# Low part of the second low-rank product: 128 rows of both operands in place of 64

## The chip, the core and the metric

The kernel runs on one core of one Trainium2 chip. A core has five engines that work side by side: TensorE (matrix products, in the profile PE, with its weight loads as PEld), VectorE (DVE), ScalarE (ACT), GpSimd (POOL) and SyncE (SP), which issues the transfers. The metric is the device time of one execution in microseconds, the median of several runs. The profile is one further execution, taken with the hardware profiler.

## The reference, cut to what matters

The reference is one step of a two-layer backbone for 640 tokens (128 context tokens, 512 latent tokens) of width 1024. Layer 0 mixes tokens with a gating MLP, layer 1 with a bidirectional RWKV-7 scan; each is followed by an MLP. The change touches layer 1, where decay and in-context rate are made by two low-rank products for each direction `d`:

```python
z = w0[i, d] + tanh(xw @ w1[i, d]) @ w2[i, d]          # w1: 1024 x 64, w2: 64 x 1024
decay = exp(-exp(-softplus(-z) - 0.5))
a = sigmoid(a0[i, d] + (xa @ a1[i, d]) @ a2[i, d])      # a1: 1024 x 64, a2: 64 x 1024
```

The second product of each, `... @ w2` and `... @ a2`, has an inner size of 64. Its result, for all 1024 channels and 640 tokens, goes into the scan together with `r`, `k` and `v`.

## The kernel before, in words

Activations lie with channels on the 128 partitions, so width 1024 is 8 tiles of 128 channels (two heads each) by 640 tokens. A product in float32 is made of products of two rounded parts: each operand is split into a high part and the rest, the low part, and high by high, high by low and low by high are summed in PSUM. `split` (lines 85 to 90) and `fill` (98 to 101) do so: ScalarE copies to the rounded type, VectorE subtracts.

`rwkv_project` (line 749) makes what the scan needs. The first low-rank products (lines 790 to 795) give, for each kind, 128 rows: 64 of direction 0 and 64 of direction 1. `hidden` (806 to 816) makes of them one operand `hw` per direction with 128 rows. For direction 0 rows 0 to 63 hold the high part and rows 64 to 127 the low part of the same 64 values; for direction 1 the halves change places. The second weights come from the host with their 64 rows written twice (line 1989), so that a tile `l2` has the same 64 rows in both halves.

`lora2` (895 to 915) makes the second products for one channel tile `t`. ScalarE rounds the weights to `hi` (898) and VectorE makes the low part `lo` (899), both on all 128 rows. Then, for each direction, kind (`tw` decay, `ta` rate) and half of 320 tokens, two products go into one bank of PSUM: line 911, `hi` by `hw` on 128 rows, which is high by high and high by low in one, and line 912, `lo` by `hw` on those 64 rows that hold the high part. Line 913 takes the bank out on ScalarE with a tanh (`ACT tw L913` and `ACT ta L913` in the profile). The pool `pv` has two such banks (line 869). `lora2` is a generator, and its steps are put between other products.

The loop of the stage (1046 to 1082) goes over `t` = 0 to 8. One turn starts `lora2`, makes the products of `r` for tile t (`rmm`, 48 matmuls at line 114, out to `rps`) and those of `v` for an earlier part (`vmm`, 60 matmuls at line 1038, out to `vps`), with the steps of `lora2` between, and then `finish` (978), which spreads the norms of `k` by a product (line 981, `rbps`), makes `kk` (985) and calls `prep` (917) for both directions: from `tw` a running sum on VectorE (920, 921), exponentials on ScalarE (927, 929), small copies on GpSimd (932), the products `KR` (938, 940) and `IT` (947, 950, 952), stored to DRAM for the scan. The pool `ep` has two buffers for `tw` and three for `ta` (870), so a `tw` can be written only when line 952 has read the one of the same direction of the tile before.

Into the same stage GpSimd puts the first part of the scan: a substitution of 31 steps (lines 1128 and 1130), released three steps at a time by `next(core)` and `core.send` (995, 1017) between the instructions of `finish`.

The order on each engine is not that of the code line by line. The framework orders the instructions ahead of time by priority and by when it takes each to be ready, with costs of its own for each instruction; `high_priority` blocks move some ahead. On the chip every engine then works through its own queue in that order and waits on semaphores. Transfers are issued on SyncE's queue.

Of the kernel before, what the change touches and what calls it, by code (L numbers as in the profile page):

```python
# [28 lines left out]
def tile_trunk(ctx: ExitStack, tc: tile.TileContext, a: dict):  # L29
# [3 lines left out]
    pe = nc.tensor  # L33
# [709 lines left out]
    def fl(x):  # L743
        return x.rearrange("p c t -> p (c t)")
# [4 lines left out]
    def rwkv_project(norm, dr, PC, bon, unwind, core, ATs, go):  # L749
        with ExitStack() as es:  # L750
# [19 lines left out]
            for hf, (t0, t1) in enumerate(HS):  # L770
                x0, x1 = XS[hf]
                a0, a1 = max(x0, 1), min(x1, T - 1)
                with urgent(hf):
                    bc = norm.rstd(hf)
                    for k in range(KT):
                        h, x = hs[k], xx[k]
# [13 lines left out]
                for j, w, ps in zip((1, 4, 5), lws, pl):  # L790
                    for k in range(KT):
# [3 lines left out]
                                  start=(k == 0), stop=(k == KT - 1))  # L795
# [99 lines left out]
            def lora2(raw, tiles):  # L895
                hi = ev_.tile([P, 4, P], F32R, "lh", "l2h")
                lo = ev_.tile([P, 4, P], F32R, "ll", "l2l")
                act.copy(hi.rearrange("p a b -> p (a b)"), raw[:, 0:512])
                vec.tensor_tensor(out=lo.rearrange("p a b -> p (a b)"), in0=raw[:, 0:512],
                                  in1=hi.rearrange("p a b -> p (a b)"), op=ALU.subtract)  # L900
                yield
                for d in range(2):
                    a0 = 64 * d
                    for x, tag in enumerate(("tw", "ta")):
                        z = ep.tile([P, 10, 64], F32, tag, tag)
                        tiles[d, x] = z
                        hw = hid[x][d]
                        for h in range(2):
                            sl = slice(320 * h, 320 * h + 320)
                            ps = pv.tile([P, 512], F32, "z", "zps")[:, 0:320]  # L910
                            pe.matmul(ps, hi[:, 2 * x + d], hw[:, sl], start=True, stop=False)
                            pe.matmul(ps, lo[a0:a0 + 64, 2 * x + d], hw[a0:a0 + 64, sl], start=False, stop=True)
                            act.activation(out=fl(z)[:, sl], in_=ps, func=AF.Tanh, scale=0.5,  # L913
                                           bias=hb[:, 2 * x + d, tiles["t"]:tiles["t"] + 1])
                            yield
# [130 lines left out]
            for t in range(KT + 1):  # L1046
                z = iter(())
                if t < KT:
                    tiles = {"t": t}
                    rl, rr = nxt  # L1050
                    z = lora2(rl, tiles)
                    next(z)
                    rk = rmm(t, rr, z)
                    if t == 0:
                        khat()
                    if t < KT - 1:
                        nxt = ahead(t + 1)
# [801 lines left out]
    for h in range(2):  # L1859
        a0 = 64 * h  # L1860
# [162 lines left out]
```

## Time and profile before

| | us |
|---|---|
| median of 3 runs (2079.52 to 2081.85) | 2079.96 |
| profiled execution, its own time | 2069.75 |
| span in that profile, first to last instruction | 2067.9 |
| TensorE busy in the span | 1938.2 |
| VectorE busy | 1344.3 |
| ScalarE busy | 842.3 |
| GpSimd busy | 543.9 |
| first and last start of the products of lines 911 and 912 | 824.7 to 1043.7 |

The granted clock of TensorE over the span was 0.944 of full speed. A row of a group gives line, engine, operation, what is written and read, the shape (partitions by elements), and a count, then busy us and mean ns, or, for one tile, minimum, median and maximum ns. A row of the timeline gives the start in us from the start of the span, a length in us and, in brackets, idle time of the engine just before and what ended it. Matmuls overlap in part, so two starts in a row say more than a length. A few of the matmuls are missing from the records.

### The profile page before, as it was taken

To read this page: it belongs to the slowest core of one execution; us is meant where nothing else is said; L and a number is where in the kernel's file an instruction comes from. 1 tells how busy PE (TensorE), PEld (TensorE's weight loads), DVE (VectorE), ACT (ScalarE), POOL (GpSimd) and SP (SyncE) were. 2 spreads that over 40 slices of the span, in tenths; PEclk is the share of its full clock that TensorE was granted. 3 is DMA by queue.
4 is the path that set the end of the run, shared out by engine and by line. 5 is a ranking of instruction groups with operands and counts; after the bars stand their busy time and mean duration, and the time that the engine had idled before them with its cause. 6 is when DMAs were issued, how large, how long until landed. Compare 5 with 4: busy or idle time off the path is not lost.

```text
span 2067.9 us, 39399 instructions
## 1 busy us (share of the span) xinstructions
PE 1938.2 (94%) x15594; PEld 1685.9 (82%) x15594; DVE 1344.3 (65%) x2652; ACT 842.3 (41%) x1945; POOL 543.9 (26%) x793
## 2 busy tenths in 40 slices
PE   6999999999999879898869999999999999999997
PEld 4766999999999759777757766767787899999997
DVE  5444556746465696776787587787757666556564
ACT  5322442413233245554524545454434633333241
POOL 0000003213020110377642284465301023121210
PEclk9999999999999889998778999998799999999999
DMA  8777121241413114454564445452241221312121
GB/s 283 267 259 249 62 72 61 82 143 62 153 54 129 63 65 156 126 172 145 175 192 141 151 145 172 158 174 67 77 132 57 92 75 59 102 62 92 64 80 52
DMA packets 124441, 254.60 MB, mean 123 GB/s; under 512 B 24416, under 2 KB 63968, under 8 KB 124128
## 3 DMA queue, kind: packets, MB, share of 16 engines
q1 hardware_dynamic: 123824, 251.62, 37.6%
q8 instruction: 123, 2.02, 0.4%
q14 instruction: 62, 0.51, 0.1%
q10 hardware_dynamic: 432, 0.46, 0.1%
HBM read 214.67 MB, written 45.22 MB: 126 GB/s over the span
## 4 chain that ended last, share of the span: by engine, by line
PE 78%; DVE 11%; ACT 4%; issue 3%; POOL 3%; DMA 1%; SPq 0%; DVEq 0%; ACTq 0%; POOLq 0%
PE fmps L114 27%; PE fmps L611 13%; PE zps L311 5%; PE p L1197 4%; PE wops L1467 4%; PE vps L1038 3%; PE za L1326 2%; PE za L1313 2%; PE rps L114 2%; PE sy L1340 2%; DVE slo L453 1%; PE sy L1321 1%; PE trps L1219 1%; PE adaps L1453 1%; DVE cs L603 1%
## 5 line engine op out<-in xcount | busy, mean ns | idle before, releaser
L611 PE MATMUL fmps<-th,shi 128*128 128x320 f32 (+2 forms) x1208 | 270.5, 312 | 9.8 <-ACT th L561 4.1
L284 DVE SCALAR_TENSOR_TENSOR x<-fmps,mod,x 128x128 f32<-128x128 f32 (+2 forms) x153 | 74.7, 527 | 254.1 <-PE fmps L114 254.1
L611 PEld LDWEIGHTS fmps<-th,shi 128*128 128x128 f32 x1208 | 202.8, 189 | 18.8 <-ACT th L561 5.7
L452 ACT CAST shi<-wraw 128x1024 fp32r<-128x1024 f32 (+1 forms) x132 | 108.9, 845 | 219.4 <-PE fmps L114 144.5
L611 PE MATMUL fmps<-th,slo 128*128 128x320 f32 (+2 forms) x604 | 187.2, 310 | 0.0
L114 PE MATMUL fmps<-ahi,shi 128*128 128x256 f32 (+1 forms) x704 | 166.4, 310 | 0.0
L114 PE MATMUL fmps<-ahi,slo 128*128 128x256 f32 (+1 forms) x704 | 165.5, 309 | 0.0
L114 PE MATMUL fmps<-alo,shi 128*128 128x256 f32 (+1 forms) x704 | 165.4, 309 | 0.0
L453 DVE TENSOR_TENSOR slo<-wraw,shi 128x1024 fp32r<-128x1024 f32 (+1 forms) x132 | 133.3, 1013 | 42.5 <-ACT shi L452 42.3
L611 PE MATMUL fmps<-th,w1s 128*128 128x320 f32 (+2 forms) x972 | 150.0, 312 | 4.0 <-DVE cs L658 3.4
L611 PEld LDWEIGHTS fmps<-th,w1s 128*128 128x128 f32 x972 | 144.6, 189 | 6.6 <-DVE cs L658 5.2
L114 PEld LDWEIGHTS fmps<-ahi,shi 128*128 128x128 f32 x704 | 128.0, 188 | 4.2 <-issue 2.5
L114 PEld LDWEIGHTS fmps<-alo,shi 128*128 128x128 f32 x704 | 128.6, 188 | 0.0
L114 PEld LDWEIGHTS fmps<-ahi,slo 128*128 128x128 f32 x704 | 128.5, 188 | 0.0
L592 POOL TENSOR_TENSOR bs<-th 128x640 f32<-128x640 f32 x8 | 17.0, 2133 | 421.5 <-DVE alo L562 305.9
L1128 POOL TENSOR_TENSOR inv<-inv 128x220 f32<-128x220 f32 (+29 forms) x217 | 98.1, 452 | 109.7 <-DVE inv L1121 57.6
L114 PE MATMUL fmps<-ahi,w1s 128*128 128x256 f32 (+1 forms) x640 | 124.1, 309 | 0.0
L475 POOL TENSOR_TENSOR s<-wraw 128x512 f32<-128x512 f32 x24 | 32.5, 1356 | 329.7 <-DMA wraw<-w 283.6
L1197 PE MATMUL p<-W,IT 128*128 128x256 f32 x320 | 106.6, 443 | 9.8 <-DVE B L1212 5.9
L611 PEld LDWEIGHTS fmps<-th,slo 128*128 128x128 f32 x604 | 114.2, 189 | 0.0
L1130 POOL TENSOR_TENSOR inv<-inv 128x220 f32<-128x220 f32 (+29 forms) x217 | 106.4, 490 | 16.9
L452 ACT CAST w1s<-wraw 128x1024 fp32r<-128x1024 f32 (+1 forms) x66 | 54.9, 836 | 131.4 <-PE fmps L114 81.8
(337 smaller groups left out, 4925.6 us busy)
## 6 DMA issues: line engine op xcount, KB each, us to landing
wraw<-w SPq DMA_DIRECT2D x126, 512.0 KB, 3.6
wraw<-ada SPq DMA_DIRECT2D x64, 512.0 KB, 4.5
W<-dKR SPq DMA_DIRECT2D x80, 256.0 KB, 3.5
adaw<-adac SPq DMA_DIRECT2D x32, 512.0 KB, 4.6
dKR<-zero SPq DMA_DIRECT2D x32, 320.0 KB, 6.2
dKR<-KR SPq DMA_DIRECT2D x32, 320.0 KB, 4.1
dIT<-IT SPq DMA_DIRECT2D x16, 640.0 KB, 3.2
IT<-dIT SPq DMA_DIRECT2D x80, 128.0 KB, 3.0
```

The source lines that it names most:

```text
L114: pe.matmul(ps[:, PS0 + t0:PS0 + t1], w, x[:, t0:t1], start=start, stop=stop)
L284: vec.scalar_tensor_tensor(out=X[n][:, t0:t1], in0=ps[:, t0 - r[0]:t1 - r[0]], scalar=mod[l][:, which, n, g:g + 1], in1=X[n][:, t0:t1], op ...
L311: pe.matmul(pss[i], x[:, i * P:(i + 1) * P], w[:, kq * 512:(kq + 1) * 512], start=(k == 0 and j == 0), stop=(k == KT - 1 and j == 2))
L452: act.copy(dst[0], x)
L453: vec.tensor_tensor(out=dst[1], in0=x, in1=dst[0], op=ALU.subtract)
L611: pe.matmul(ps, u, v, start=first and z == 0, stop=last and z == 2, **kw)
L1038: pe.matmul(pss[i // 2][:, i % 2], x[:, i * P:(i + 1) * P], w[:, kq * 256:(kq + 1) * 256], start=(k == 0 and j == 0 and i % 2 == 0), stop= ...
L1128: eng.tensor_tensor(out=tv, in0=LA[:, s + 1:32, s:s + 1].to_broadcast([P, n, m]), in1=LX[:, s:s + 1, c0:c1].to_broadcast([P, n, m]), op=AL ...
L1130: eng.tensor_tensor(out=LX[:, s + 1:32, c0:c1], in0=LX[:, s + 1:32, c0:c1], in1=tv, op=ALU.subtract)
L1197: pe.matmul(ps[:, :, 2 * e:2 * e + 2].rearrange("p h s t -> p h (s t)"), IT[:, e], W[:, :, 2 * e:2 * e + 2].rearrange("p h s t -> p h (s t ...
L1313: pe.matmul(za[a0:a0 + 64, 0], W[:, h, 3 * e], RZ[:, ti, h, c], start=True, stop=True)
L1467: pe.matmul(ps, u, v, start=start and j == 0, stop=stop and j == 2)
```

## The change

The low part of the weights, `lo`, is multiplied by `hw` on all 128 rows instead of the 64 that hold the high part. Since `lo` has the same weights in both halves of its rows, the product takes in low by low as well. Line 911, the split of the weights, the banks, the evictions and the loop stay as they are.

```diff
                 for d in range(2):
-                    a0 = 64 * d
                     for x, tag in enumerate(("tw", "ta")):
                         z = ep.tile([P, 10, 64], F32, tag, tag)
                         tiles[d, x] = z
...
                             pe.matmul(ps, hi[:, 2 * x + d], hw[:, sl], start=True, stop=False)
-                            pe.matmul(ps, lo[a0:a0 + 64, 2 * x + d], hw[a0:a0 + 64, sl], start=False, stop=True)
+                            pe.matmul(ps, lo[:, 2 * x + d], hw[:, sl], start=False, stop=True)
                             act.activation(out=fl(z)[:, sl], in_=ps, func=AF.Tanh, scale=0.5,
                                            bias=hb[:, 2 * x + d, tiles["t"]:tiles["t"] + 1])
                             yield
```

## The prediction

> **What bounds the kernel now.** First the page, for the share of each engine, then the windows around the lines of the change, then the instructions that write the tile `zps`, the timeline of TensorE, the waits of the stage, and the chain that ended last.
>
> ```profile
> span 2067.9 us, 39399 instructions
> ...
> PE 1938.2 (94%) x15594; PEld 1685.9 (82%) x15594; DVE 1344.3 (65%) x2652; ACT 842.3 (41%) x1945; POOL 543.9 (26%) x793
> ```
>
> TensorE is busy for 94% of the span, but the change touches one stage of it. The two products in question run once per tile of two heads (8), direction (2), kind (2: decay, rate) and token half (2), 64 times each, between 824.7 and 1044 us:
>
> ```profile
> L911 PEld LDWEIGHTS zps<-hw,l2h x64: 186/188/333, 824.7 to 1043.4; 128*128 128x128 f32 x64
> L911 PE MATMUL zps<-hw,l2h x64: 306/309/635, 824.8 to 1043.4; 128*128 128x320 f32 x64
> L912 PEld LDWEIGHTS zps<-hw,l2l x64: 182/183/334, 825.0 to 1043.7; 64*128 64x128 f32 x64
> L912 PE MATMUL zps<-hw,l2l x64: 303/410/632, 825.0 to 1043.7; 64*128 64x320 f32 x64
> L913 ACT ACTIVATE tw<-zps,hb x32: 513/527/534, 825.7 to 1041.6; 128x320 f32<-128x320 f32 x32
> L913 ACT ACTIVATE ta<-zps,hb x32: 527/528/534, 829.7 to 1044.2; 128x320 f32<-128x320 f32 x32
> ```
>
> Both stream 320 columns; the median of the 64-row one is 410 ns against 309. In the windows (length, then busy us and count of PE, PEld, DVE, ACT, POOL, then granted clock) the stage from 825 to 1045 us has 192.26 of 220 us of TensorE, so 27.7 us in which it waits, and a clock of 0.86:
>
> ```profile
> 885.00:945.00 60.00, 50.53 (x304) 41.97 (x302) 42.86 (x38) 30.49 (x50) 49.87 (x60) 0.89 0.55 162
> 825.00:1045.00 220.00, 192.26 (x1165) 161.45 (x1164) 159.55 (x136) 113.03 (x183) 135.11 (x170) 0.86 0.53 159
> ```
>
> So here TensorE is the busiest engine, but not alone: GpSimd has 49.87 of the 60 us from 885. The chain says the same (shares of these 220 us):
>
> ```profile
> by line: PE vps L1038 22.6%; PE rps L114 15.8%; issue 8.6%; PE zps L912 7.6%; POOL AT L1128 5.7%; PE zps L911 4.3%; POOL inv L1130 4.0%; POOL PC L932 2.5%; PE bops L1013 2.3%; PE rbps L114 2.3%; DVE IT L952 2.0%; POOL k L993 1.9%; PE aps L9
> ```
>
> The changed line holds 7.6% of it, 16.7 us, and its partner L911 4.3%, 9.5 us.
>
> **The change part by part.** It removes no instruction and adds none, moves none, and issues no DMA. The low part `lo` and the operand `hw` exist on all 128 rows already, and L911 waits for all of `hw` just ahead, so I see no new wait: cost nothing, and nothing that would need cover. What changes is how 64 matmuls and their 64 weight loads run. Their price stands in the distance from start to start on TensorE, first at full clock, then at half clock (start, length, engine, line, tile):
>
> ```profile
> 865.01 0.56 PE L114 MATMUL rps<-ahi,whi 128*128 128x256 f32 x2
> 865.41 0.31 PE L911 MATMUL zps<-hw,l2h 128*128 128x320 f32 x1
> 865.65 0.41 PE L912 MATMUL zps<-hw,l2l 64*128 64x320 f32 x1
> 865.99 0.39 PE L114 MATMUL rps<-alo,whi 128*128 128x256 f32 x1
> ...
> 872.24 0.46 PE L114 MATMUL rps<-ahi,wlo 128*128 128x256 f32 x2
> 872.54 0.46 PE L114 MATMUL rps<-ahi,whi 128*128 128x256 f32 x2
> 872.83 0.47 PE L114 MATMUL rps<-alo,whi 128*128 128x256 f32 x2
> ```
>
> ```profile
> 913.83 0.47 PE L911 MATMUL zps<-hw,l2h 128*128 128x320 f32 x1
> 914.22 0.63 PE L912 MATMUL zps<-hw,l2l 64*128 64x320 f32 x1
> 914.79 0.58 PE L1038 MATMUL vps<-wlo,ahi 128*128 128x256 f32 x1
> ```
>
> ```profile
> 936.49 0.74 PE L114 MATMUL rps<-ahi,whi 128*128 128x256 f32 x2
> 937.03 0.73 PE L114 MATMUL rps<-alo,whi 128*128 128x256 f32 x2
> ```
>
> From L911 to L912 is 0.24 us, from L912 to what follows 0.34: 0.58 us for a pair. Two products of L114 (256 and 384 columns, together 640, as a pair has) go from 872.24 to 872.54 and to 872.83, so 0.295 us, all on 128 rows. At half clock a pair takes 914.79 - 913.83 = 0.96 us, and 640 columns take 937.03 - 936.49 = 0.54. So a pair on 128 rows should cost 0.285 us less, 0.42 where the clock is low. The weight loads show where the time goes:
>
> ```profile
> 832.29 0.19 PEld L911 LDWEIGHTS zps<-hw,l2h 128*128 128x128 f32 x1
> 832.40 0.31 PE L911 MATMUL zps<-hw,l2h 128*128 128x320 f32 x1
> ...
> 832.64 0.18 PEld L912 LDWEIGHTS zps<-hw,l2l 64*128 64x128 f32 x1 [0.16 <-issue]
> 832.64 0.41 PE L912 MATMUL zps<-hw,l2l 64*128 64x320 f32 x1
> ...
> 832.98 0.19 PEld L1038 LDWEIGHTS vps<-whi,ahi 128*128 128x128 f32 x1 [0.16 <-issue]
> ```
>
> L911's load starts 0.11 us before its matmul, behind the matmul before it; L912's load starts with its own matmul, at 832.64, after an idle loader, and so does the load that follows. It is the change between 64 and 128 rows that holds the loads back, and it goes twice per pair.
>
> The Trainium skill speaks against this: TensorE: Matmul & The Clock Gate, LDWEIGHTS, says that the rows of a weight load do not enter its time, and its closing table that a product on 32 rows takes as long as one on 128. By that the sum is zero. The lengths of the loads agree (182 against 186 ns), the distances between starts do not. TensorEngine Tiling (Array Packing), Key Properties, says that changing the tiling mode drains TensorE, which agrees with both distances and by which the whole 0.285 us goes.
>
> Sum on TensorE: 64 x 0.285 = 18.2 us. Bounds of this term: 0, if the new load does not run ahead either, and 64 x 0.42 = 27 us, if all pairs stood at half clock. I take 18.2, as the clock of 0.86 is nearer to full.
>
> How much reaches the end is the real question. Who waits for these products, and what they wait for (us in total, times, longest):
>
> ```profile
> ACT tw L913 <- DVE IT L952: 20.6, 7, 5.6
> ACT ta L913 <- PE zps L912: 13.5, 24, 4.1
> DVE tw L920 <- ACT tw L913: 10.5, 6, 3.8
> PE zps L911 <- ACT tw L913: 8.7, 2, 6.2
> DVE kk L985 <- PE rbps L114: 4.1, 5, 1.1
> ACT tw L913 <- PE zps L912: 1.9, 6, 0.5
> ```
>
> Of 64 evictions on ScalarE 24 + 6 = 30 waited for L912; the other 34 found it done, held up by other work. Seven waited for `IT` L952 of the tile before, whose `tw` buffer they overwrite: the stage is a ring from eviction over VectorE, ScalarE and GpSimd back to the next eviction, and a pair that ends earlier in it often only waits longer:
>
> ```profile
> 1014.49 1.49 DVE L952 TENSOR_TENSOR IT<-IT,tw 128x1280 f32<-128x1280 f32 x1
> ...
> 1016.08 0.95 ACT L913 ACTIVATE tw<-zps,hb 128x320 f32<-128x320 f32 x2 [3.33 <-DVE IT L952]
> ...
> 1016.66 0.64 PE L911 MATMUL zps<-hw,l2h 128*128 128x320 f32 x1 [6.17 <-ACT tw L913]
> ```
>
> So 30 x 0.285 = 8.6 us is what ScalarE can get earlier. About half of it I let through, 4.3 us: VectorE waits for a tanh six times only, and from 885 to 945 GpSimd sets the pace with work that needs no `zps`. The other way out is TensorE's order: `rps`, `vps` and `rbps` behind the pairs start earlier, and of this VectorE's 4.1 us of waiting for `rbps` is the end; I take 0.7 us of it, since in the code 60 `vps` products lie between the pairs and `rbps`. What is late next is ScalarE: a pair with its two L114 neighbours takes 0.98 us now (865.01 to 865.99), would take 0.70, and ScalarE needs 0.53 for its eviction, beside other work.
>
> Sum: 4.3 + 0.7 = 5.0 us off; with all of both, 8.6 + 4.1 = 12.7. The profiled execution would go from 2069.75 (span 2067.9 and 1.85 around it) to 2064.7. The median of the runs, 2079.96, stands 10.2 above it, so I subtract from that: 2075.0 us.
>
> **The rivals.** A change of 0.2% of the median, 4.2 us, is about what a measurement tells from none.
>
> *Hidden.* The ring and GpSimd take back nearly all; TensorE is idle 18 us longer. For it: 20.6 us of waits for L952, 49.87 of 60 us of GpSimd. Against it: 30 evictions that did wait. With 1.5 us gained: 2078.5.
>
> *All of TensorE's part.* The pairs and what is queued behind them set the pace: up to 18.2 us, 2061.8; with 12.7, 2067.3. For it: 12% of the chain on L911 and L912. Against it: 27.7 us in which TensorE waits.
>
> *Rows cost nothing.* The new load also starts with its matmul; 2079.96. Against it: every load of L911.
>
> *A worse order.* The order of each engine is worked out ahead, and it is not that of the code:
>
> ```profile
> 906.99 0.90 PE L911 MATMUL zps<-hw,l2h 128*128 128x320 f32 x2 [3.96 <-ACT l2h L898]
> ...
> 908.99 0.90 PE L912 MATMUL zps<-hw,l2l 64*128 64x320 f32 x2
> ```
>
> In the code L912 follows each L911. Were the new shape planned as shorter, L911 of the next tile would stand on TensorE's queue ahead of `vps` or `rps` and wait for its PSUM bank there, as at 1016.66, for 6.17 us with all that is behind it. One more such wait eats the gain (+1.2 us); from two it is slower: 12.3 - 5.0 = 7.3, 2087.3. For it: two such waits exist. Against it: the readiness of L911 does not change.
>
> **How the numbers follow.** Forecast (4.2 to 9 us faster) 0.40, all of TensorE's part 0.10: faster 0.50. Hidden 0.32, rows cost nothing 0.05: same 0.37. Worse order 0.13: slower. The range reaches from the 12.7 us, 2067, to 2084, leaving out the worse order (0.13) and the upper part of the large gain (0.05). The forecast's own range is 2071 to 2075.8.
>
> **What would show it.** Right: L912 lists 128x320, median near 309 ns; its load starts about 0.1 us ahead; from L911 to L911's second follower 0.30 us; busy TensorE in the stage falls by 15 us or more, `ACT ta L913 <- PE zps L912` below 13.5 us, and what ends the stage comes about 5 us earlier. Wrong: the distance stays at 0.34, or `ACT tw L913 <- DVE IT L952` grows by what the pairs lost, or a new wait of `zps` L911 over 3 us, or a stage behind 1045 us that differs as much as this one.

## The result and the profile after

The changed kernel takes 2066.18 us (median of 4 runs, 2065.02 to 2067.19), the kernel before 2079.74 (4 runs, 2079.33 to 2081.85). The ratio is 0.9937, with an interval of 0.9924 to 0.9949: 13.6 us, or 0.65%, faster. The forecast was 2075.0 with a range from 2067 to 2084. The direction was right, the gain was almost three times the forecast of 5.0 us, and the time lies 0.8 us below the range.

From line 903 on, line numbers of the changed kernel are one lower: 910, 911 and 912 are 911, 912 and 913 of before. In the stage of the change the order of the instructions is the same on every engine, line by line, and behind it only a few products and loads of the recurrence that start close together change places in the records. So the rival of a worse order is out: nothing was planned anew.

The page of the changed kernel, span and busy time by engine:

```profile
span 2063.2 us, 39399 instructions
...
PE 1918.9 (93%) x15594; PEld 1683.1 (82%) x15594; DVE 1345.6 (65%) x2652; ACT 839.9 (41%) x1945; POOL 547.7 (27%) x793
```

TensorE loses 19.3 us of 1938.2; all counts are as before. The instructions that write or read `zps` in the changed kernel (count; shortest, median and longest ns; first and last start; form):

```profile
L910 PE MATMUL zps<-hw,l2h x64: 302/318/636, 824.3 to 1031.4; 128*128 128x320 f32 x64
L911 PEld LDWEIGHTS zps<-hw,l2l x64: 186/189/338, 824.3 to 1031.5; 128*128 128x128 f32 x64
L911 PE MATMUL zps<-hw,l2l x64: 302/309/547, 824.5 to 1031.7; 128*128 128x320 f32 x64
...
L912 ACT ACTIVATE ta<-zps,hb x32: 502/529/560, 828.5 to 1032.3; 128x320 f32<-128x320 f32 x32
```

The low product lists 128 rows and a median of 309 ns in place of 410. From the first high product to the last `ta` eviction is what I call the stage below: 824.3 to 1032.3, so 207.9 us with all digits, against 824.8 to 1044.2, 219.4 us, before. The stage is 11.5 us shorter. The timeline of TensorE in the changed kernel (start, length, engine, line, tile), and that of its weight loads:

```profile
890.09 0.31 PE L910 MATMUL zps<-hw,l2h 128*128 128x320 f32 x1
890.23 0.30 PE L911 MATMUL zps<-hw,l2l 128*128 128x320 f32 x1
890.37 0.28 PE L114 MATMUL rps<-alo,whi 128*128 128x256 f32 x1
890.49 0.31 PE L910 MATMUL zps<-hw,l2h 128*128 128x320 f32 x1
```

```profile
889.95 0.19 PEld L910 LDWEIGHTS zps<-hw,l2h 128*128 128x128 f32 x1
890.09 0.19 PEld L911 LDWEIGHTS zps<-hw,l2l 128*128 128x128 f32 x1
890.23 0.19 PEld L114 LDWEIGHTS rps<-alo,whi 128*128 128x128 f32 x1
```

The loads now start one product ahead: that of 911 at 890.09, 0.14 us before its matmul at 890.23, and the follower's likewise. In the timeline of the kernel before, this row comes behind the four that the prediction shows from 865.01 on:

```profile
866.22 0.31 PE L911 MATMUL zps<-hw,l2h 128*128 128x320 f32 x1
```

So from a high product to the second product behind its pair it was 866.22 - 865.41 = 0.81 us, and it is now 890.49 - 890.09 = 0.40. What follows a pair is not the same everywhere, so each pair has to be compared with the pair at the same place in the other trace. 38 places have it at full clock and without a wait in both: there the three steps had medians of 0.239, 0.340 and 0.224 us and now have 0.152, 0.147 and 0.120, and a pair with all three is shorter by a median of 0.385 us and a mean of 0.367 (0.380 and 0.365 over 37 places of the two repeated profiles below). The third step is the one that the prediction left out.

The windows around the stage (length; busy us and count of PE, PEld, DVE, ACT and POOL; granted clock; DMA share; GB/s), of the changed kernel:

```profile
825.00:1033.00 208.00, 168.14 (x1162) 154.48 (x1160) 159.53 (x136) 110.35 (x183) 138.29 (x170) 0.88 0.55 166
```

TensorE is busy for 168.14 us in place of 192.26, and idle for 39.9 in place of 27.7: about half of what it saved shortened the stage, and half stands as waiting. What waits now (waiting engine and line, releaser; total us, times, longest):

```profile
ACT ta L1004 <- POOL ta L1002: 16.6, 6, 4.4
PEld zps L910 <- ACT tw L912: 16.2, 8, 8.4
ACT tw L912 <- DVE IT L951: 16.0, 5, 5.2
...
PE zps L910 <- ACT tw L912: 13.5, 6, 7.8
...
ACT ta L912 <- PE zps L911: 5.5, 7, 2.0
```

ScalarE's wait for the low product falls from 13.5 us in 24 to 5.5 in 7, and TensorE's wait for ScalarE to empty a bank rises from 8.7 in 2 to 13.5 in 6. (In the two repeated profiles below it is 12.3 to 5.5 and 11.0 to 13.6.) The longest stands in the timeline:

```profile
1007.14 0.64 PE L910 MATMUL zps<-hw,l2h 128*128 128x320 f32 x1 [7.79 <-ACT tw L912]
```

The chain of waits through the stage has the same news (shares of these 208 us):

```profile
by line: issue 11.1%; PE rps L114 9.9%; POOL AT L1127 8.9%; POOL inv L1129 6.8%; PE vps L1037 6.5%; POOL PC L931 4.2%; DVE tw L920 3.7%; POOL ta L1002 3.7%; POOL k L992 3.4%; DMA k<-dk 2.6%; DVE KR L937 2.5%; ACT IT L946 2.4%; DVE IT L951 2
```

Before, `vps`, `rps` and the two changed lines held 50% of it, all on TensorE. Now `rps` and `vps` hold 16%, the changed lines are gone from the row, and GpSimd has the places behind them. The size of this fall is not firm: in the two repeated profiles the four shares add up to 41% before and 26% after.

### The profile page after: what moved, and what is told of

Its sections match the earlier page's. It is cut to its first block, busy times and chain, and to the rows that moved or that the text cites. A ratio compares the mean times of both kernels' runs of the same rounds, so it can differ in the third digit from the quotient of the medians.

```text
span 2063.2 us, 39399 instructions
## 1 busy us (share of the span) xinstructions
PE 1918.9 (93%) x15594; PEld 1683.1 (82%) x15594; DVE 1345.6 (65%) x2652; ACT 839.9 (41%) x1945; POOL 547.7 (27%) x793
## 4 chain that ended last, share of the span: by engine, by line
PE 75%; DVE 11%; ACT 5%; POOL 4%; issue 3%; DMA 2%; SPq 0%; ACTq 0%; DVEq 0%; POOLq 0%
PE fmps L114 27%; PE fmps L611 13%; PE zps L311 5%; PE p L1196 4%; PE wops L1466 3%; PE za L1325 2%; PE za L1312 2%; PE sy L1339 2%; DVE slo L453 2%; PE sy L1320 1%; PE adaps L1452 1%; PE trps L1218 1%; PE adaps L122 1%; DVE cs L603 1%; PE rps L114 1%
```

## The experiments

The theories that the expectations weigh: **S**, the price belongs to the change between 64 and 128 rows; against it **P**, that it belongs to any product on 64 rows. Of the length of the stage: **A**, that TensorE's own time sets it, whoever waits for the product; **B**, that only a third of what TensorE saves reaches the end and the rest of the 13.6 us is a difference between single executions; **R**, that the ring through the evictions sets it, so that it matters whether `tw` or `ta` comes earlier; **C**, that the stretches at half clock set it. The stage is taken as above, and the time at half clock is counted within it. In the stage the order on TensorE is that of the kernel before in all rows but three: "high products grouped", "no low product" and "sum on VectorE", which were planned anew. One execution each:

| kernel | stage us | TensorE busy | idle | at half clock | span |
|---|---|---|---|---|---|
| before | 219.4 | 192.5 | 26.9 | 61.4 | 2067.9 |
| before, again | 220.6 | 192.3 | 28.3 | 61.7 | 2076.8 |
| high products grouped | 219.5 | 190.8 | 28.7 | 58.0 | 2074.7 |
| both products on 64 rows | 222.1 | 196.1 | 26.0 | 76.2 | 2076.2 |
| one direction changed | 211.5 | 179.9 | 31.5 | 55.9 | 2065.7 |
| decay changed | 211.1 | 178.6 | 32.5 | 45.2 | 2064.0 |
| rate changed | 211.0 | 180.9 | 30.1 | 55.5 | 2066.9 |
| changed, 32 `vps` on 64 rows | 214.0 | 181.1 | 32.8 | 55.0 | 2068.8 |
| changed | 207.9 | 168.8 | 39.1 | 48.9 | 2063.2 |
| changed, again | 207.9 | 168.7 | 39.2 | 49.0 | 2060.8 |
| changed, no low product | 205.5 | 165.0 | 40.5 | 64.9 | 2066.6 |
| changed, sum on VectorE | 199.4 | 168.2 | 31.2 | 47.8 | 2050.8 |

**Both kernels again.** No edit of the kernel before; in the changed one, only the unused line `a0 = 64 * d` stands again, so that its line numbers are those of before; it does so in all further kernels made from the changed one.

> The kernel before, unchanged, profiled once more, to see in which stage one execution differs from another. Theory A (TensorE sets the pace of the stage of the two low-rank products, so that most of the 15 us that it lost there reach the end): the stage again ends about 11 to 12 us later than in the changed kernel, and whatever else differs lies behind 1045 us; the execution takes 2070 to 2082 us. Theory B (only a third of it reaches the end, 4 to 6 us, and the rest of the 13.6 us is a difference of single executions in other stages): the stage ends only 4 to 6 us later than in the changed kernel in this profile.

> The change once more, with every other line at its place. Theory A: 2066 us, ratio 0.9935 +- 0.001, and the stage ends 11 to 12 us ahead of that of the kernel before. Theory B: a ratio of 0.997 to 0.998 in a second set of runs.

Before, again: 2078.61 us, one run, beside 17 others with a median of 2079.83. Changed, again: 2065.66 (5 runs, 2060.68 to 2066.37), ratio 0.9933 with an interval of 0.9909 to 0.9958. The windows of the kernel before, again:

```profile
825.00:1045.00 220.00, 191.38 (x1163) 160.40 (x1162) 158.76 (x136) 111.80 (x182) 134.85 (x170) 0.86 0.53 158
```

The stage repeats: 219.4 and 220.6 us before, 207.9 and 207.9 after. What differs between executions of one kernel lies behind it. From the first to the last product of `za`, in the recurrence that follows, the two profiles of before take 496.5 and 502.9 us, the two of after 501.6 and 497.6. The profile on which I predicted was taken in an execution 10 us shorter than the median, and in that part it is 6.4 us shorter than the repeat; only 3 of the 17 runs beside this one were under 2075 us. So 11.5 to 12.7 of the 13.6 us come from the stage, against B. The remaining 1 to 2 us lie within the spread behind it, and no run settles them.

**One direction, one kind.** Half of the 64 products take 128 rows: those of the first direction, those of the decay, or those of the rate.

```
-  pe.matmul(ps, lo[a0:a0 + 64, 2 * x + d], hw[a0:a0 + 64, sl], ...)
+  pe.matmul(ps, lo[ks, 2 * x + d], hw[ks, sl], ...)
   # one direction: ks = slice(0, 128) if d == 0 else slice(64, 128)
   # decay alone:   ks = slice(0, 128) if x == 0 else slice(a0, a0 + 64)
   # rate alone:    ks = slice(0, 128) if x == 1 else slice(a0, a0 + 64)
```

> The low part's product on 128 rows for direction 0 only, on 64 rows for direction 1: 32 of the 64 products changed, the order of every engine as before. Theory A: half of the gain, 6.8 us, ratio about 0.9967 (0.995 to 0.998), and TensorE busy in the stage falls by about 8 us. Theory B: 2 to 3 us, within the noise. A gain that does not follow the count (all or nothing) would speak for a chance shift of the stage against the clock or against GpSimd, theory C.

> The low part's product on 128 rows for the decay (tw) only: 32 of the 64 products, order as before. Theory A: half of the stage's gain whatever the kind, 5 to 6.5 us (stage about 213 us). Theory R (the ring through tw: running sum, exponentials, IT sets the pace): most of the gain, 9 us or more, here, and little from the other kind.

> The low part's product on 128 rows for the in-context rate (ta) only: the other 32 products, order as before. Theory A: 5 to 6.5 us off the stage (about 213 us). Theory R: 2 us or less. If the two halves together give much more or less than the whole (11.5 us), the gain is not a sum over products but goes in steps, by the granted clock's windows (theory C): half-clock time in the stage should then differ by whole windows of 3.4 us between these two kernels.

One direction: 2066.67 us (7 runs), ratio 0.9946, 0.9927 to 0.9965. Decay alone 2065.76, rate alone 2068.64, one run each beside a median of 2078.78. The groups show the halves with one direction, and then come the windows with decay alone and with rate alone:

```profile
L912 PE MATMUL zps<-hw,l2l x64: 303/410/632, 826.8 to 1037.5; 128*128 128x320 f32 x32, 64*128 64x320 f32 x32
```

```profile
825.00:1036.00 211.00, 178.29 (x1164) 155.76 (x1163) 159.99 (x136) 111.97 (x182) 137.26 (x170) 0.89 0.56 164
```

```profile
825.00:1036.00 211.00, 180.42 (x1164) 157.95 (x1163) 160.38 (x136) 110.95 (x183) 136.37 (x170) 0.87 0.56 164
```

Whichever half it is, TensorE loses 11.4 to 13.9 us and the stage 7.9 to 9.6, about two thirds. That is more than the half of the gain that the expectations by A had put down (5 to 6.5 us; a ratio of 0.9967 for one direction). The other half then takes 9.8 to 12.1 us off TensorE, but only 3.1 to 3.6 off the stage, a third or less. It does not matter which kind comes earlier, against R. With decay alone the clock is low for 45.2 us and with rate alone for 55.5, and the stages have 211.1 and 211.0: against C. What counts is how much of TensorE's time goes, with a return that falls.

**High products grouped.** From the kernel before: both halves' banks are taken at once, then line 911 runs for both, then line 912 for both, then the two evictions.

```
+  pzs = [pv.tile([P, 512], F32, "z", "zps")[:, 0:320] for h in range(2)]
+  for ps, sl in zip(pzs, sls):
       pe.matmul(ps, hi[:, 2 * x + d], hw[:, sl], start=True, stop=False)
+  for ps, sl in zip(pzs, sls):
       pe.matmul(ps, lo[a0:a0 + 64, 2 * x + d], hw[a0:a0 + 64, sl], start=False, stop=True)
```

> The products on 64 rows as before, but the two halves of the tokens put together: line 911 for both halves, then line 912 for both, so that TensorE goes from 128 to 64 rows and back 32 times in place of 64. If the change of rows is what costs (0.1 us going in, 0.2 us coming out): 9 us less on TensorE, two neighbours of line 912 about 0.15 us apart, and by theory A some 7 us faster, ratio 0.9967; by theory B 2 to 3 us. If every product on 64 rows costs its 0.285 us by itself: neighbours 0.34 us apart, no change from the pairing. An order that the framework works out anew may add or take a few us.

2077.88 us (10 runs), ratio 1.0005, 0.9983 to 1.0026: no change. But the planned order did not follow the code. In 53 of the 64 cases a low product still stood right behind a high one, at medians of 0.239 and 0.340 us as before, and two low ones followed each other in 7 places in place of 4. The number of changes was hardly lowered, so this run says nothing on its question.

**Both products on 64 rows.** From the kernel before; the high product leaves out the product of the weights' high part with the tokens' low part.

```
-  pe.matmul(ps, hi[:, 2 * x + d], hw[:, sl], start=True, stop=False)
+  pe.matmul(ps, hi[a0:a0 + 64, 2 * x + d], hw[a0:a0 + 64, sl], start=True, stop=False)
```

> From the kernel before, line 911 too takes only the 64 rows that hold the high part (the product of the weights' high part with the activations' low part is left out), so that a pair is 64 rows and 64 rows between neighbours of 128; every engine's order as before. Theory S (the price is the change between 128 and 64 rows, one going in and one coming out): the distance from line 911 to line 912 falls to about 0.15 us, the one from line 912 to the next neighbour stays at 0.34, the way into line 911 grows by about 0.1; the pair costs as much as before, and the stage ends where it did (219 us from the first to the last start of line 911, +- 3). Theory P (each product on 64 rows pays by itself): both distances at 0.3 or more, 18 us more on TensorE, and a stage that is longer by 5 to 14 us.

2077.95 us, one run, beside a median of 2078.78. The groups of the two products, and a pair in TensorE's timeline:

```profile
L911 PE MATMUL zps<-hw,l2h x64: 302/410/633, 826.5 to 1047.8; 64*128 64x320 f32 x64
L912 PE MATMUL zps<-hw,l2l x64: 299/306/468, 826.7 to 1048.1; 64*128 64x320 f32 x64
```

```profile
867.37 0.38 PE L114 MATMUL rps<-alo,whi 128*128 128x256 f32 x1
867.68 0.41 PE L911 MATMUL zps<-hw,l2h 64*128 64x320 f32 x1
867.94 0.30 PE L912 MATMUL zps<-hw,l2l 64*128 64x320 f32 x1
868.17 0.44 PE L114 MATMUL rps<-alo,whi 128*128 128x384 f32 x1
```

The 410 ns move to line 911, which now comes first behind 128 rows; line 912, on 64 rows as before, falls to 306. A product on 64 rows behind another one pays nothing in its length. The distances, at the 31 places that are at full clock and without a wait here and before: 0.264 us from the product ahead to 911, 0.251 to 912, 0.233 to the follower and 0.224 to the one behind it; before they were 0.175, 0.238, 0.340 and 0.223. Place by place the median difference of the whole way is 0.00 us (mean 0.04). Twice as many products on 64 rows, as many changes, the same price: S holds. (The stage is 1.5 to 2.7 us longer, but the clock was low in it for 14.5 us more.) The 0.15 us that I expected between the two was wrong: the first one's own late start lies in it.

**32 products of `vps` on 64 rows.** From the changed kernel: of the 480 products of line 1037, those with the tokens' low part for the first 128 tokens take 64 rows, which leaves out half of that sum. No tanh reads these; their banks are emptied into `vs`.

```
-  pe.matmul(..., x[:, i * P:(i + 1) * P], w[:, kq * 256:(kq + 1) * 256], ...)
+  pe.matmul(..., *(y[:64 if j == 1 and i == 0 else P] for y in (x[:, ...], w[:, ...])), ...)
```

> From the changed kernel, 32 other products of the same stage are put on 64 rows between neighbours of 128: those of line 1038 of the activations' low part for the first 128 tokens (half of their sum is left out); every engine's order as before. They are not waited for by the tanh. By the price per pair this puts 32 x 0.28 = 9 us back on TensorE. Theory A (TensorE's own time sets the pace of the stage, whoever waits for it): three quarters of it come back, the stage is 6 to 7 us longer than in the changed kernel (207 us), and the runs take 2072 +- 2 us. Theory R (the gain came through the tanh's waits for line 912 alone): the stage is longer by 2 us or less.

2072.11 us (10 runs), ratio 0.9974, 0.9959 to 0.9989. TensorE's timeline and the windows:

```profile
857.21 0.28 PE L1038 MATMUL vps<-whi,ahi 128*128 128x256 f32 x1
857.42 0.38 PE L1038 MATMUL vps<-whi,alo 64*128 64x256 f32 x1
857.73 0.38 PE L1038 MATMUL vps<-wlo,ahi 128*128 128x256 f32 x1
857.96 0.28 PE L1038 MATMUL vps<-whi,ahi 128*128 128x256 f32 x1
```

```profile
826.00:1040.00 214.00, 180.89 (x1165) 160.69 (x1163) 159.26 (x136) 110.79 (x182) 135.52 (x170) 0.87 0.55 163
```

Steps of 0.21, 0.31 and 0.23 us stand where plain neighbours of 256 columns have a median of 0.12: three late starts, 0.39 us. Over the stage 12.3 us are back on TensorE, 0.38 for each of the 32, and the stage is 6.1 us longer, half of them. That is the same half that the change took off, put back in a product that no tanh reads. So TensorE's time counts wherever in its queue it is spent, and not only in the products for which the 30 evictions waited. The way to the end may still lead over the tanh, for the pairs stand in the same queue behind these products: ScalarE's waits for them rise from 5.5 to 9.7 us, 8.4 and 1.3 (`ACT ta L913 <- PE zps L912: 8.4, 11, 2.1`).

**Two products on 64 rows in a row, in the last matrices.** From the changed kernel: in one of the three products of chunk 4 of the last layer's second matrix (line 671) both halves of the columns take 64 rows, which leaves out half of its sum. It makes 35 groups between products on 128 rows, 29 of two products and 6 of one, 64 products in all.

```
-  mmh(ps, chunk(w, k)[wi], ss[k][xi], ...)
+  mmh(ps, *(y[:64 if l == 1 and k == 4 and z == 1 else P] for y in (chunk(w, k)[wi], ss[k][xi])), ...)
```

> From the changed kernel, in the second half of layer 1's MLP, where TensorE is busy for nearly all of the time, one of 24 steps of a product (line 671: weights' high part by activations' low part, fifth chunk) takes 64 rows (half of that step's sum is left out); every engine's order as before. It makes 35 groups between neighbours of 128 rows, 29 of two products (256 and 384 columns) one behind the other and 6 of one. Theory S (the price is the change of rows, about 0.33 us for in and out together): 35 x 0.33 = 11.6 us, and as TensorE sets the pace there, all of it reaches the end: 2078 +- 2.5 us; the second of two products starts as soon after the first as on 128 rows. Theory P (each product on 64 rows pays): 64 x 0.33 = 21 us, 2087. If the price exists only in the stage of the change: 2066.

2073.64 us (10 runs), ratio 0.9994 to the kernel before, 0.9969 to 1.0019. That is below the 2078 +- 2.5 that S had asked for, but in this set the kernel before stands at 2074.25, 5.5 us lower than in the first; by the ratios, 0.9994 against 0.9933 and 0.9937, this kernel is 12 to 13 us slower than the changed one. Three rows of its timeline ("x2" is two products of 384 and 256 columns), and the windows behind the last `za` product, of this kernel and then of the changed one:

```profile
1711.02 0.46 PE L114 MATMUL fmps<-ahi,shi 128*128 128x256 f32 x2
1711.40 0.56 PE L114 MATMUL fmps<-alo,shi 64*128 64x256 f32 x2
1711.89 0.56 PE L114 MATMUL fmps<-ahi,slo 128*128 128x256 f32 x2
1712.29 0.45 PE L114 MATMUL fmps<-ahi,shi 128*128 128x256 f32 x2
```

```profile
1556.00:2071.50 515.50, 490.79 (x3174) 467.83 (x3171) 314.44 (x545) 183.98 (x335) 82.80 (x55) 0.98 0.23 71
```

```profile
1560.00:2063.00 503.00, 478.05 (x3184) 468.37 (x3183) 312.29 (x549) 184.70 (x339) 85.31 (x55) 0.98 0.22 73
```

The three rows take 1712.29 - 1711.02 = 1.27 us, where three times the 0.295 of the prediction would be 0.885: 0.385 more for going to 64 rows and back, with two products between. For all groups that would be 35 x 0.385 = 13.5 us. From the last `za` to the end it is 516.4 us against 503.0, 13.4 more, of which the windows show 12.7 as TensorE's. Here TensorE is busy for 95% of the time, and all of it reaches the end. The same price for two products on 64 rows as for one, where P had asked for nearly twice as much: S again.

**No low product.** From the changed kernel: line 911 goes, and with it the weights' low part; the high product closes the sum.

```
-  pe.matmul(ps, hi[:, 2 * x + d], hw[:, sl], start=True, stop=False)
-  pe.matmul(ps, lo[:, 2 * x + d], hw[:, sl], start=False, stop=True)
+  pe.matmul(ps, hi[:, 2 * x + d], hw[:, sl], start=True, stop=True)
```

> From the changed kernel, the product of line 912 is left out altogether (the low part of the second weights is not used), which takes another 64 x 0.147 = 9.4 us from TensorE in the stage; the framework orders the instructions anew. Theory A with about a half let through: the stage (207.9 us in the changed kernel) ends 3 to 5 us earlier, 203 to 205 us. If what is left of the stage is set by the ring of VectorE, ScalarE and GpSimd: 207 +- 1.5 us.

2068.40 us, one run, beside a median of 2074.25. The stage has 205.5 us, only 2.4 fewer than with the low products, and on the border of the two forecasts. But TensorE's time fell by 3.8 us alone, where 64 x 0.15 = 9.6 are removed: the clock was low for 64.9 us in place of 48.9. The waits that lead, from 825 to 1045 us:

```profile
ACT ta L1005 <- POOL ta L1003: 24.7, 5, 6.1
...
PE zps L911 <- ACT tw L913: 16.6, 7, 7.2
```

Both are longer than in the changed kernel (19.5 and 13.5 in the same window). So this run found little left to gain by the products of this line; how much of that is the ring, how much the lower clock and how much the new order, one run does not tell.

**The sum of the rates on VectorE.** From the changed kernel: one of ScalarE's longest waits in both lists above is for the sum of the two directions' rates on GpSimd (line 1002 there). That sum goes to VectorE. The computation is the same.

```
-  nc.gpsimd.tensor_tensor(out=fl(s), in0=fl(s), in1=fl(tas[1]), op=ALU.add)
+  vec.tensor_tensor(out=fl(s), in0=fl(s), in1=fl(tas[1]), op=ALU.add)
```

> From the changed kernel, the sum of the two rates (line 1003) goes from GpSimd to VectorE, 8 instructions in all. In the changed kernel ScalarE waits for it 19.5 us in 7 places, with the evictions of the two products queued behind that wait, and TensorE waits 13.5 us for those evictions. On GpSimd it takes 1.5 to 2.9 us, products of the same size on VectorE 0.8. If this wait sets the pace now: the stage 5 to 10 us shorter, 2058 to 2063 us. If VectorE (168 of 220 us busy) or the ring through it does: no change, 2066, or up to 3 us slower.

2051.31 us (4 runs, 2050.25 to 2052.63), ratio 0.9897, 0.9881 to 0.9913. All four are below all nine runs of the changed kernel (2060.68 to 2067.19), which were taken in other sets. The kernel before was 5.5 us lower in this set than in the first, so the ratios say more than the times: 0.9897 against 0.9933 and 0.9937, some 8 us faster than the changed kernel. By its time alone it would lie below the 2058 to 2063 us that were forecast. The group in the changed kernel, then here, then the windows, and the waits from 825 to 1045 us:

```profile
L1002 POOL TENSOR_TENSOR ta<-ta x8: 1533/2712/2823, 835.3 to 1039.1; 128x640 f32<-128x640 f32 x8
```

```profile
L1003 DVE TENSOR_TENSOR ta<-ta x8: 800/823/1290, 840.4 to 1031.5; 128x640 f32<-128x640 f32 x8
```

```profile
825.00:1025.00 200.00, 168.21 (x1167) 153.92 (x1165) 154.91 (x144) 111.48 (x183) 131.69 (x163) 0.88 0.59 175
```

```profile
ACT tw L913 <- DVE IT L952: 13.9, 8, 3.4
...
ACT ta L1005 <- DVE ta L1003: 6.7, 3, 5.1
...
PE zps L911 <- ACT tw L913: 4.8, 3, 3.0
```

2.7 us of GpSimd become 0.8 of VectorE, eight times. TensorE is as busy as in the changed kernel, 168.2 against 168.1 us, and the stage is 8.5 us shorter: its idle time falls from 39.1 to 31.2. TensorE's wait for ScalarE to empty a bank falls from 13.5 to 4.8 us. So a good part of the waiting in the changed kernel was the ring from eviction to eviction through ScalarE and GpSimd. The order was planned anew here, so the 8.5 us are those of the move with its order; and the move was not made in the kernel before, so whether it would have given as much there is open.

## Why the prediction was right and wrong

**The cause** was right: the change between 64 and 128 rows holds the loads back. The row of line 911 at 309 ns, its load 0.14 us ahead, and the two runs that moved the number of products apart from the number of changes (both on 64 rows; two in a row) show it. The rival that rows cost nothing falls. The Trainium skill (TensorE: Matmul & The Clock Gate, LDWEIGHTS) says that the rows of a weight load do not enter its length, and the trace agrees, 182 against 186 ns; but by that rule alone no time would have been gained. The Trainium skill (TensorEngine Tiling (Array Packing), Key Properties) says that a change of the tiling mode drains TensorE, and the late starts after every change of rows agree with it; the drain itself no trace here shows.

**The price of a pair**, 0.285 us, was too small: I counted two distances, up to the start of the first follower, and set them against 0.295. These two fell as I had said, by 0.088 and 0.192 us. But the follower of the follower starts late too, 0.224 us in place of 0.120. With it a pair costs 0.367 (mean) to 0.385 us (median) more, 64 times that is 23.5 to 24.6 us, and not 18.2. The row that shows it, 866.22, was the next one of the view that I quoted. TensorE's busy time in the stage fell by 23.7 us (192.5 to 168.8), where I asked for 15 or more, about what the pairs come to. The clock was low for 12.5 us less as well; what part that had in it these runs do not separate.

**What reaches the end** is the step that failed: "30 x 0.285 = 8.6 us is what ScalarE can get earlier. About half of it I let through". That, with 0.7 us for `rbps`, let 5.0 of 18.2 us through, 27%. Measured are 11.5 to 12.7 us of 23.7, about half. I had counted only the pairs whose eviction waited for line 912, as if the time of the other 34 were lost. But a shorter pair also moves up everything queued behind it on TensorE: the 32 `vps` products, which no tanh reads, cost half their time as well. By which of the products behind them the time reaches the end, the runs do not separate. The chain of before pointed this way, with 50% on TensorE's `vps`, `rps` and the two lines (41% in the repeat); I went by the waits in place of it. The 0.7 us "of VectorE's 4.1" is part of the same mistake.

**The rivals.** "Hidden" is out, and so is "all of TensorE's part" as a whole: 18.2 us, 2061.8, is more than came. Its lower price, 2067.3 with 12.7 us, was the nearest of all that stood there, and I had given it 0.10 together with the upper one. That TensorE waited for 27.7 us in the stage was weak evidence against it: 27.7 us of idle time stood beside a saving of 23.7, and half of it came through. The order stayed as it was.

**What is late next** was named rightly. ScalarE's evictions and the ring behind them take the other half: `PE zps L910 <- ACT tw L912` went from 8.7 to 13.5 us, with 7.8 the longest, the new wait over 3 us that I had put down as a sign against me. It came together with the gain, as what ends it. `ACT tw L912 <- DVE IT L951` did not grow (20.6 to 16.0); `ACT ta L1004 <- POOL ta L1002` rose from 14.4 to 16.6, one of ScalarE's two longest now, and moving that one sum off GpSimd gave 8.5 us more of the stage.

**The base** was handled rightly: taking the gain off the median and not off the profiled 2069.75 us, which was an execution short by 6.4 us in a part that the change does not touch.

## What to carry to other kernels

A lone product on 64 rows between products on 128 costs three late starts, not one: compare the starts up to the second follower with those of plain neighbours, since the lengths show only part. Where the operand has further rows that may be added to the sum, fill them, or put products of one height side by side in the order that the engine really runs. To judge how much of a saving on a busy engine comes through, look at the share of the chain that runs over that engine's whole queue, not only at the consumers that waited for the changed instruction. Here it was 50% and 41% in two profiles, and about half came through; that is one case and no rule, for the first half of the products gave two thirds of their saving and the second a third or less. Then look for the next wait on the ring, for that is where the other part of it went.

## What the runs showed of the hardware

- A change of rows and back costs TensorE 0.37 to 0.385 us with one product of 320 columns between (mean and median over 38 places), 0.38 with one of 256 (12.3 us for 32), and 0.385 with two products of together 640 columns (1.27 against 0.885 us). I had expected 0.285 and had not expected the product after the next one to pay.
- Lengths mislead here: the first product on 64 rows lists 410 ns for 309 and the first on 128 rows behind it 0.1 us more as well (0.38 for 0.28 in the `vps` rows), together 0.2 us of the 0.385. A second product on 64 rows lists 306 ns.
- Removing 64 products left the clock low for longer, 64.9 against 48.9 us, and TensorE's busy time almost as it was (165.0 against 168.8). One profile without them, two with them (48.9 and 49.0); why the clock fell is open.
- A sum of 128x640 in float32 took GpSimd a median of 2.7 us and VectorE 0.82.
